# Hybrid decoder layer on Trainium2: forgetting attention with its pools opened once, keys loaded by block on SP's queue, output-projection tiles laid singly between its items, and casts on other engines

## The chip, the cores and the metric

One core of a Trainium2 chip runs the whole program. The metric is device time in microseconds (us), from runs of the unchanged kernel: median 3135.35 of three (3137.12, 3130.89, 3135.35). Engines are named as in the profile: PE (TensorE matmul), PEld (its weight load), DVE (VectorE), ACT (ScalarE), POOL (GpSimd), SP (SyncE, which here only issues transfers). ACTq and SPq are the streams of transfers that ACT and SP issue. TensorE's clock has two levels, 1.2 and 2.4 GHz; the profile prints the granted share, 0.5 to 1.0.

## The reference, cut to what matters

One layer, 2048 positions, width 1024. Four groups of heads (RWKV-7, mLSTM, sliding-window attention, forgetting attention) read one normalised input; their outputs stand side by side in `y` (2048 x 1024) and one output projection maps them back. The change touches the last group and that projection.

```
def _fox(z, b_f):                       # 4 heads of 64
    q, k, v, f_pre = split(z)
    c = cumsum(log_sigmoid(f_pre + b_f), axis=1)
    s = q_i . k_j / 8 + c_i - c_j       # j <= i, else -inf
    return softmax(s) @ v

y = concatenate([y_a, y_b, y_c, y_d])
x = x + rmsnorm(y @ w_out, norm_mix_post)
h = rmsnorm(x, norm_ffn_pre)
gate, up = split(h @ ffn_w_up)          # then conv, GELU, product, w_down, rmsnorm, residual
```

## The kernel before

**Stages.** `stage1` does the input projection and the RWKV heads, and as fillers beside them the other groups. `stage2` does forgetting attention ("fox") and the output projection. `stage_n` does the channel mixer: the up products (L1580), then the down product. Positions are cut into NC = 4 chunks of C = 512 and these into 4 sub-tiles of 128 rows, so there are 16 tiles t; chunk c holds tiles 4c to 4c+3.

**Fox items.** An item is (head h, chunk c of queries). The order, number by number, is 0, 1: heads 0, 1 of chunk 0; 2, 3: heads 0, 1 of chunk 1; 4, 5: heads 2, 3 of chunk 0; 6, 7: heads 2, 3 of chunk 1; 8 to 11: chunk 2; 12 to 15: chunk 3. An item has a front and a back. The front (`fox_front`, L1281) loads queries and the c+1 key blocks of 512 (`fox_load`, L1264: tiles `ka` and `kb`), forms the logits for 128 queries and a block at a time (L1291, L1292, and L1294 for the mask), takes the minimum on DVE (L1295), and ends in a transposition of the row minima (L1308) that ACT copies into `QB` (L1309). It has 4(c+1) steps. The back (`fox_back`, L1312) forms transposed logits for 128 keys a step (L1324, L1325, L1327), exponentiates on ACT (L1329, tile `fP`), splits the result into two halves of 16 bits (L1331 the rounded one, on ACT; L1333 the rest, on POOL for every third step and on DVE for the others; tile `fhl`), and multiplies with the values two steps later (L1339). It has 4(c+1)+2 steps. `fox` (L1364) interleaves the back of one item with the front of the next; with `first=True` the front of its first item runs alone, before anything of its back.

**Pools.** Fox's pools are opened twice: for items 0 to 5 with 5 key buffers and 2 PSUM banks for logits, and for items 6 to 15 with 8 key buffers and 4 banks. After item 5 the iterator of items is empty, so no front runs beside item 5's back.

**Output tiles.** `o_front` (L1435) loads 128 rows of `y` on SP (L1440), takes their maximum (L1442), splits into 16-bit halves in tile `hl` (L287, L288) and transposes these by transfers on SP (L290, `yt`). `o_back` (L1451) loads a tile of `x` on ACT's queue into the single buffer `xr` (L1456), runs 96 matmuls of 256 columns (L276 to L278), normalises (L1464 to L1469), adds `x` on POOL (L1470), stores it (L1471), and makes the transposed input of the channel mixer, `V` (L298, L301, L284, L285, L290), through the same two buffers `hl`. V of chunks 0 and 1 lies in a pool on the right side of SBUF; V of chunks 2 and 3 in a pool on the left that takes the memory of fox's pools when these close. `combine(0)` (L1475) then forms sums and differences of V of chunks 0 and 1 on POOL, DVE and ACT (L1485 to L1489, tile T0, in the same left pool); the first up product needs them and the first weights `Wup` (L1562, L1563).

**What sets the order.** Each engine runs its own instructions in a fixed order, and each of SP, ACT and POOL issues its transfers in that order too. The order is made at compile time (L1736): program order is the priority, and a simulated timeline lets later work go ahead where earlier work isn't ready. So L888 to L891 put tiles 0 to 3 behind item 7 and tiles 4 to 7 behind item 11, and L905 tiles 8 to 15 behind all of fox, but where they run is read from the trace.

Of the kernel before, what the change touches and what calls it, by code (L numbers as in the profile page):

```python
# [22 lines left out]
NC = T // C  # L23
# [116 lines left out]
class Trunk:  # L140
# [723 lines left out]
    def stage2(self):  # L864
        with ExitStack() as ck, ExitStack() as co:
            self.cr_.close()
            self.fk = self.pool(ck, "fk")
            items = [[(h, c) for h in hs] for c, hs in ((0, (0, 1)), (1, (0, 1)), (0, (2, 3)), (1, (2, 3)), (2, range(4)), (3, range(4)))]
            with ExitStack() as cf:
                self.fox_pools(cf, 5, 3, 5, 2)  # L870
                self.fox_setup()
                self.fox_items = iter(items[0] + items[1] + items[2])
                self.fox(3, True)
                self.fill_heads(1)
                self.fox(3)
            self.twice = False
            self.cm_.close()
            self.cf.close()
            self.cu.close()
            with ExitStack() as cf:  # L880
# [12 lines left out]
            keep = self.pool(self.ctx, "keep_n")  # L893
# [5 lines left out]
            self.sn = self.pool(self.ctx, "small_n", bufs=4)  # L899
# [333 lines left out]
    def fox_pools(self, ctx, nk, npe, nh, nps):  # L1233
# [3 lines left out]
        self.psf = self.pool(ctx, "ps_a", bufs=nps, space=PSUM)  # L1237
        self.fbufs = nk, npe, nh
# [25 lines left out]
    def fox_load(self, hp, c):  # L1264


        nc, wk = self.nc, self.fw
        qa, qb = wk.tile([P, C], F32R, name="qa", bufs=2), self.QB[self.loads % 3]
        self.loads += 1
        nc.scalar.dma_start(out=qa.bitcast(F32), in_=self.qF[hp][c][:, :])  # L1270
        nc.scalar.dma_start(out=qb[0:64].bitcast(F32), in_=self.qF[hp][c][0:64])
        nc.gpsimd.memset(qb[64:66].bitcast(F32), 0.0)
        K = []
        for b in range(c + 1):
            ka, kb = wk.tile([P, C], F32R, name="ka", bufs=self.fbufs[0]), wk.tile([68, C], F32R, name="kb", bufs=self.fbufs[0])
            nc.scalar.dma_start(out=ka.bitcast(F32), in_=self.kA[hp][b][:, :])
            nc.scalar.dma_start(out=kb.bitcast(F32), in_=self.kB[hp][b][:, :])
            K.append((ka, kb))
        return qa, qb, K

    def fox_front(self, hp, c):  # L1281

        nc, small, psf = self.nc, self.sf, self.psf
        qa, qb, K = self.ops = self.fox_load(hp, c)
        mx = small.tile([P, NSUB, 4], F32, name="fmx", bufs=3)
        for i in range(NSUB):
            isl = slice(i * P, (i + 1) * P)
            for b in range(c + 1):
                n = C if b < c else (i + 1) * P
                ps = psf.tile([P, C], F32, name="psf")  # L1290
# [15 lines left out]
        ps = psf.tile([P, C], F32, name="psf")  # L1306
# [5 lines left out]
    def fox_back(self, hp, c, ops):  # L1312

        nc, wk, small, psf = self.nc, self.fw, self.sf, self.psf
# [5 lines left out]
        def num(s):  # L1320
            b, ks = s // NSUB, slice(s % NSUB * P, s % NSUB * P + P)
            o = max(0, s - 4 * c) * P
            ps = psf.tile([P, C], F32, name="psf")
# [7 lines left out]
            nc.scalar.copy(out=h[:, 0, o:], in_=e[:, o:])  # L1331
            eng = nc.gpsimd if s % 3 == 1 else nc.vector
# [53 lines left out]
    def o_setup(self, ctx):  # L1386
        nc = self.nc
        self.U2 = [self.u2p.tile([P, 2, KT, C], F16, name=f"V{c}") for c in range(2)] + [None] * (NC - 2)
# [15 lines left out]
    def o_tiles(self, c):  # L1404
        if c == 0:
            self.of = self.o_front(0)
        for t in range(c * NSUB, (c + 1) * NSUB):
            self.of = self.o_back(t, self.of, t + 1 if t + 1 < NC * NSUB else None)
# [331 lines left out]
```

## Time and profile before

| what | us |
|---|---|
| median of three runs | 3135.35 |
| the profiled execution, whole | 3123.52 |
| its span, first to last instruction | 3121.4 |
| PE busy in the span | 2751.2 |
| from the last matmul of item 5 to the back of item 6 | 28.7 |
| fox from there to its end | 339.3 |
| from the end of fox to the first up product | 123.8 |

The profiled execution lies 11.8 us under the median of the runs. The spans of the last three lines are read from the timeline of PE; the rows stand below. A row of a timeline gives start and duration in us, engine, line, operation, output and inputs, and in brackets how long the engine had been idle and what released it.

### The profile page before, as it was taken

How to read it: one execution, taken by the hardware profiler on the slowest of the kernel's cores; microseconds unless marked ns; L12 is line 12 of the kernel's file. 1: busy time of each engine (PE TensorE's matmuls, PEld its weight loads, DVE VectorE, ACT ScalarE, POOL GpSimd, SP SyncE). 2: the span in 40 equal slices, each digit the busy share in tenths (PEclk: the TensorE clock that was granted, in tenths of full speed). 3: DMA queues.
4: the chain of work that ended last, by engine and by line, in shares of the span. 5: the costliest groups of instructions: out<-in, count | busy, mean ns of one | idle time of the engine just before them, and what ended most of it. 6: DMA issues, size and time to landing. Idle time of an engine off the chain costs nothing.

```text
span 3121.4 us, 45097 instructions
## 1 busy us (share of the span) xinstructions
PE 2751.2 (88%) x17374; PEld 1656.7 (53%) x17374; DVE 1707.9 (55%) x3512; ACT 1043.6 (33%) x1844; POOL 848.8 (27%) x989
## 2 busy tenths in 40 slices
PE   1499889999998989699885578999999998999998
PEld 0145577777776876577664233444444443444443
DVE  3465466557775655466766576466555554622120
ACT  2343222345452223356673322222222222522020
POOL 1153221223323332122224333333323332010110
PEclk9699889999988998799997799999999999999999
DMA  6441223244652365484425332111111111832120
GB/s 178 98 115 58 83 72 106 81 106 129 166 130 78 90 171 169 119 169 118 129 63 133 102 121 87 49 68 56 53 54 61 54 55 43 275 124 92 56 85 21
DMA packets 341398, 313.67 MB, mean 100 GB/s; under 512 B 217600, under 2 KB 271232, under 8 KB 338368
## 3 DMA queue, kind: packets, MB, share of 16 engines
q1 hardware_dynamic: 265856, 238.42, 27.2%
q10 hardware_dynamic: 75328, 72.39, 7.7%
q8 instruction: 136, 2.23, 0.3%
q14 instruction: 78, 0.64, 0.1%
HBM read 187.86 MB, written 89.56 MB: 89 GB/s over the span
## 4 chain that ended last, share of the span: by engine, by line
PE 47%; issue 11%; DVE 9%; DMA 8%; POOL 5%; ACT 1%; SPq 0%; ACTq 0%; POOLq 0%; DVEq 0%
PE psd L1675 10%; PE psb L1580 7%; PE psc L1580 4%; PE psa L1580 4%; PE pso L1339 1%; POOL S L1539 1%; DMA rd<-in_w_dn 1%; PE psf L276 1%; PE psf L278 1%; PE psf L277 1%; PE psf L268 1%; POOL F L1617 1%; PE psf L266 1%; PE psf L267 1%; PE psg L276 1%
## 5 line engine op out<-in xcount | busy, mean ns | idle before, releaser
L1580 PEld LDWEIGHTS <-Wup 128*128 128x128 f16 x3696 | 365.9, 99 | 537.8 <-issue 86.0
L1675 PE MATMUL psd<-Wd,f 128*128 128x512 f16 x2112 | 458.1, 380 | 8.2 <-ACT Wd L1660 8.1
L1580 PE MATMUL psb<-T,Wup 128*128 128x512 f16 x1584 | 382.6, 391 | 49.0 <-DVE up L1583 44.2
L1675 PEld LDWEIGHTS <-f 128*128 128x128 f16 x2112 | 207.0, 98 | 259.3 <-issue 6.6
L1580 PE MATMUL psa<-V,Wup 128*128 128x512 f16 x1056 | 248.8, 383 | 28.8 <-ACT Wup L1562 23.7
L276 PE MATMUL psg<-Wo,yt 128*128 128x256 f16 x512 | 145.7, 285 | 57.1 <-DMA yt<-hl 54.5
L1595 ACT ACTIVATE X<-psa,wm 128x512 f32<-128x512 f32 x44 | 30.2, 687 | 414.8 <-DVE p L205 244.3
L266 PE MATMUL psg<-U,hi_cm 128*128 128x512 f16 x256 | 103.8, 405 | 73.5 <-ACT hi_cm L253 73.5
L268 PE MATMUL psf<-U,lo_fm 128*128 128x256 f16 x576 | 161.5, 280 | 0.0
L266 PE MATMUL psf<-U,hi_fm 128*128 128x256 f16 x576 | 161.5, 280 | 0.0
L267 PE MATMUL psf<-U,hi_fm 128*128 128x256 f16 x576 | 161.4, 280 | 0.0
L278 PE MATMUL psg<-Wo,yt 128*128 128x256 f16 x512 | 143.7, 283 | 7.5 <-DMA yt<-hl 7.5
L277 PE MATMUL psg<-Wo,yt 128*128 128x256 f16 x512 | 145.7, 285 | 0.0
L1619 DVE TENSOR_REDUCE mF<-F 128x2 f32<-128x1024 f32 x44 | 53.7, 1221 | 165.7 <-POOL F L1617 165.6
L276 PE MATMUL psf<-hi_fv,U 128*128 128x256 f16 (+1 forms) x512 | 137.8, 276 | 3.6 <-ACT zc L779 3.6
L1683 DVE TENSOR_SCALAR od<-psd,sf 128x512 f32<-128x512 f32 x16 | 12.0, 750 | 233.6 <-PE psd L1675 229.1
L277 PE MATMUL psf<-lo_fv,U 128*128 128x256 f16 (+1 forms) x512 | 138.1, 276 | 0.0
L278 PE MATMUL psf<-hi_fv,U 128*128 128x256 f16 (+1 forms) x512 | 137.8, 276 | 0.0
L1580 PE MATMUL psc<-T,Wup 128*128 128x512 f16 x528 | 131.9, 381 | 0.0
L1295 DVE TENSOR_REDUCE fmx<-psf 128x1 f32<-128x512 f32 (+3 forms) x160 | 96.0, 606 | 64.8 <-PE psf L1292 38.8
L268 PE MATMUL psg<-U,lo_cm 128*128 128x512 f16 x256 | 102.4, 401 | 32.5 <-DVE lo_cm L254 18.7
L1329 ACT ACTIVATE fP<-psf,ln2k 128x512 f32<-128x512 f32 (+3 forms) x160 | 97.5, 624 | 78.3 <-PE psf L1325 31.5
(446 smaller groups left out, 5979.5 us busy)
## 6 DMA issues: line engine op xcount, KB each, us to landing
raw<-in_w_up SPq DMA_DIRECT2D x22, 1024.0 KB
fD<-F SPq DMA_DIRECT2D x44, 512.0 KB
fr<-fD SPq DMA_DIRECT2D x88, 256.0 KB
rd<-in_w_dn SPq DMA_DIRECT2D x22, 512.0 KB
wdr<-in_w_dn ACTq DMA_DIRECT2D x22, 512.0 KB
zin<-zR SPq DMA_DIRECT2D x80, 128.0 KB
ka<-kA ACTq DMA_DIRECT2D x40, 256.0 KB
wst<-in_w_cm SPq DMA_DIRECT2D x17, 512.0 KB
```

Of the source, the lines that this page charges most:

```text
L266: nc.tensor.matmul(ps[:, sl], lhsT=hi[:, k, n0:n0 + nn], rhs=uh[:, k, sl], start=k == 0, stop=False)
L267: nc.tensor.matmul(ps[:, sl], lhsT=hi[:, k, n0:n0 + nn], rhs=ul[:, k, sl], start=False, stop=False)
L268: nc.tensor.matmul(ps[:, sl], lhsT=lo[:, k, n0:n0 + nn], rhs=uh[:, k, sl], start=False, stop=k == KT - 1)
L276: nc.tensor.matmul(ps, lhsT=uh[:, k, sl], rhs=hi[:, k, n0:n0 + nn], start=k == 0, stop=False)
L277: nc.tensor.matmul(ps, lhsT=uh[:, k, sl], rhs=lo[:, k, n0:n0 + nn], start=False, stop=False)
L278: nc.tensor.matmul(ps, lhsT=ul[:, k, sl], rhs=hi[:, k, n0:n0 + nn], start=False, stop=k == KT - 1)
L1295: nc.vector.tensor_reduce(out=mx[:, i, b:b + 1], in_=ps[:, :n], axis=AX.X, op=ALU.min)
L1329: nc.scalar.activation(out=e[:, o:], in_=ps[:, o:], func=AF.Exp, scale=-1.0, bias=self.ln2k)
L1339: nc.tensor.matmul(po[i // 2][:, i % 2 * 129:i % 2 * 129 + 129], lhsT=h[:, n, i * P:(i + 1) * P], rhs=self.V2[:, s, hp], start=s == 0 and ...
L1580: nc.tensor.matmul(ps, lhsT=W[:, a, n, ks], rhs=rhs[u](b, k), start=first and k == 0 and i == 0, stop=k == 3 and i == 2, skip_group_check= ...
L1619: nc.vector.tensor_reduce(out=self.mF[:, 2 * p:2 * p + 2, j:j + 1], in_=F, axis=AX.X, op=ALU.max, apply_absolute_value=True)
L1675: nc.tensor.matmul(ps, lhsT=f[:, a, sl], rhs=Wd[j][:, b, ns], start=j == 0 and k == 0, stop=j == NF - 1 and k == 2)
```

## The change

Fox's pools are opened once, for all items, with 6 key buffers; two more PSUM banks are added as a second pool once the fillers' pools close, and `fox_bank` takes banks from the two in turn. Items come from one iterator, so item 6's front runs beside item 5's back. `o_setup` (weights of the output projection, 16 loads on SP) moves ahead of items 3 to 5.

In `fox_front` the loop over key blocks becomes the outer one, and block b+1 is loaded when block b starts, on SP's queue instead of ACT's; queries stay on ACT's queue.

Of the back's steps, every third rounds on DVE instead of ACT, and every second one (before: every third) takes the rest on POOL instead of DVE.

Output tiles are laid between items: tile 0 ahead of item 6, 1 ahead of 7, 2 ahead of 8, 3 ahead of 9, 4 and 5 ahead of 10, 6 ahead of 11, none ahead of 12, 7 ahead of 13, 8 ahead of 14, 9 ahead of 15, and 10 to 15 behind all of fox. Where the second argument is given, the next tile's front isn't begun within this one's back. V of chunk 2 moves to the right-hand pool. `combine(0)` moves from behind tile 11 to behind tile 15.

```
     def stage2(self):
-            items = [[(h, c) for h in hs] for c, hs in (...)]
-            with ExitStack() as cf:
-                self.fox_pools(cf, 5, 3, 5, 2)
+                items = [(h, c) for c, hs in (...) for h in hs]
+                self.fox_pools(ck, 6, 4, 6)
                 self.fox_setup()
-                self.fox_items = iter(items[0] + items[1] + items[2])
+                self.fox_items = iter(items)
                 self.fox(3, True)
                 self.fill_heads(1)
+                self.twice = False
+                self.cm_.close()
+                self.cf.close()
+                self.cu.close()
+                self.psfs.append(self.pool(ck, "ps_a1", bufs=2, space=PSUM))
+                self.u2p = self.pool(self.c2, "u2", side="right")
+                self.o_setup(co)
                 self.fox(3)
-            self.twice = False
-            self.cm_.close()
-            self.cf.close()
-            self.cu.close()
-            with ExitStack() as cf:
-                self.fox_pools(cf, 8, 4, 6, 4)
-                self.u2p = self.pool(self.c2, "u2", side="right")
-                self.fox_items = iter([i for l in items[3:] for i in l])
-                self.fox(1, True)
-                self.o_setup(co)
-                self.fox(1)
-                for c in range(1, NC):
-                    if c > 1:
-                        self.fox(4)
-                    if c <= 2:
-                        self.o_tiles(c - 1)
-            ck.close()
+                for n, t in ((1, ((0,),)), (1, ((1,),)), (1, ((2,), 2)), (1, ((3,), 3)), (1, ((4,5),)), (1, ((6,),6)), (1, ((),)), (1, ((7,), 7)), (1, ((8, ),8)), (1, ((9,),9))):
+                    self.o_tiles(*t)
+                    self.fox(n)
...
-            for c in range(2, NC):
-                self.U2[c] = u2b.tile([P, 2, KT, C], F16, name=f"V{c}")
+            self.U2[NC - 1] = u2b.tile([P, 2, KT, C], F16, name="V3")
...
-            for c in range(2, NC):
-                self.o_tiles(c)
-                if c == 2:
-                    self.combine(0, lambda n: self.ow.tile([P, 4, W], F32, name="xs"), self.Tc[0])
+            self.o_tiles(range(10, 16), 15)
+            self.combine(0, lambda n: self.ow.tile([P, 4, W], F32, name="xs"), self.Tc[0])
...
+        def more():
+            b = len(K)
+            ka, kb = ...
+            nc.sync.dma_start(out=ka.bitcast(F32), in_=self.kA[hp][b][:, :])
+            nc.sync.dma_start(out=kb.bitcast(F32), in_=self.kB[hp][b][:, :])
+            K.append((ka, kb))
+        more()
+        return qa, qb, K, more
+    def fox_bank(self):
+        self.turn += 1
+        return self.psfs[self.turn % len(self.psfs)].tile([P, C], F32, name="psf")
...
     def fox_front(self, hp, c):
         for b in range(c + 1):
-            nc.scalar.dma_start(out=ka.bitcast(F32), in_=self.kA[hp][b][:, :])
-            nc.scalar.dma_start(out=kb.bitcast(F32), in_=self.kB[hp][b][:, :])
...
-        for i in range(NSUB):
-            for b in range(c + 1):
+            if b < c:
+                more()
+            for i in range(NSUB):
...
     def fox_back(self, hp, c, ops):
-            nc.scalar.copy(out=h[:, 0, o:], in_=e[:, o:])
-            eng = nc.gpsimd if s % 3 == 1 else nc.vector
+            if s % 3 == 2:
+                nc.vector.tensor_copy(out=h[:, 0, o:], in_=e[:, o:])
+            else:
+                nc.scalar.copy(out=h[:, 0, o:], in_=e[:, o:])
+            eng = nc.gpsimd if s % 2 == 1 else nc.vector
             eng.tensor_tensor(out=h[:, 1, o:], in0=e[:, o:], in1=h[:, 0, o:], op=ALU.subtract)
...
     def o_setup(self, ctx):
-        self.U2 = [... for c in range(2)] + [None] * (NC - 2)
+        self.U2 = [... for c in range(NC - 1)] + [None]
```

## Rows read from the trace of the kernel before

**Rows 1.** The page: the span, and the busy time of PE and DVE with their shares.

```profile
span 3121.4 us, 45097 instructions
...
PE 2751.2 (88%) x17374; PEld 1656.7 (53%) x17374; DVE 1707.9 (55%) x3512; ACT 1043.6 (33%) x1844; POOL 848.8 (27%) x989
```

**Rows 2.** Busy time of each engine in seven stretches. Columns: stretch, its length, busy us (and instructions) of PE, PEld, DVE, ACT, POOL, granted clock, share of the DMA engines, GB/s.

```profile
1216.00:1265.60 49.60, 39.37 (x243) 26.19 (x241) 22.32 (x64) 24.16 (x52) 8.52 (x11) 0.73 0.52 162
1265.60:1294.30 28.70, 8.75 (x26) 5.38 (x26) 11.87 (x30) 2.46 (x3) 0.00 (x0) 0.50 0.88 199
1294.30:1633.60 339.30, 314.33 (x2608) 243.23 (x2606) 231.97 (x447) 211.39 (x391) 94.38 (x85) 0.95 0.49 117
1633.60:1651.60 18.00, 0.01 (x1) 0.01 (x1) 10.32 (x18) 5.43 (x6) 4.95 (x7) 0.53 0.91 209
1651.60:1757.40 105.80, 59.51 (x481) 49.09 (x481) 62.12 (x93) 36.69 (x58) 46.25 (x50) 0.77 0.46 114
1757.40:1900.00 142.60, 108.28 (x447) 45.51 (x448) 97.97 (x109) 32.62 (x31) 44.11 (x49) 0.88 0.35 119
1900.00:2650.00 750.00, 715.71 (x3251) 320.40 (x3249) 414.01 (x455) 203.96 (x195) 252.62 (x192) 0.98 0.15 54
```

**Rows 3.** Timeline of PE where the pools change: the end of item 5's back, the first logits of item 6's front, the start of its back.

```profile
1264.36 1.26 PE L1339 MATMUL pso<-FV,fhl 128*128 128x129 f16 x10 [1.20 <-POOL fhl L1333]
1274.48 0.77 PE L1291 MATMUL psf<-ka,qa 128*128 128x512 f32 x1 [8.85 <-DMA ka<-kA]
1276.74 0.77 PE L1292 MATMUL psf<-kb,QB 68*128 68x512 f32 x1 [1.50 <-DMA kb<-kB]
...
1294.19 1.87 PE L1308 MATMUL psf<-c,fmr 128*2 128x128 f32 x8
```

**Rows 4.** Transfers issued on ACT's queue and on SP's around it (start, time the issue took, queue, line).

```profile
1217.11 21.12 SPq L1399 DMA_DIRECT2D Wo<-wO  x16
...
1267.65 0.48 ACTq L1270 DMA_DIRECT2D qa<-qF  x1
1268.17 0.44 ACTq L1276 DMA_DIRECT2D ka<-kA  x1
...
1576.72 0.36 ACTq L1276 DMA_DIRECT2D ka<-kA  x1
1577.15 0.32 ACTq L1277 DMA_DIRECT2D kb<-kB  x1
```

**Rows 5.** Starts of the backs of items 12 to 15 on PE (L1308 comes once an item).

```profile
1498.55 1.03 PE L1308 MATMUL psf<-c,fmr 128*2 128x128 f32 x8 [0.63 <-DVE fmr L1305]
1542.24 1.03 PE L1308 MATMUL psf<-c,fmr 128*2 128x128 f32 x8
1581.56 1.03 PE L1308 MATMUL psf<-c,fmr 128*2 128x128 f32 x8
1613.07 1.03 PE L1308 MATMUL psf<-c,fmr 128*2 128x128 f32 x8 [1.31 <-DVE fmr L1305]
```

**Rows 6.** What PE waited for from 1296 to 1634, the values' matmuls (L1339): us in total, times, longest.

```profile
PE pso L1339 <- DVE fhl L1333: 4.6, 7, 1.2
...
PE pso L1339 <- POOL fhl L1333: 3.6, 4, 1.8
```

**Rows 7.** Groups by line from 1296 to 1634: the split's instructions on DVE, ACT and POOL by shape, and one line of the tiles' matmuls. Columns: count, busy us, mean ns of one, idle before.

```profile
L1333 DVE TENSOR_TENSOR fhl<-fP,fhl 128x512 f16<-128x512 f32 x66 | 56.0, 855 | 15.2 <-ACT fhl L1331 15.1
L1331 ACT CAST fhl<-fP 128x512 f16<-128x512 f32 x98 | 58.8, 621 | 3.7 <-DVE fmx L1295 1.6 <-POOL xr L1470 0.8
L1333 POOL TENSOR_TENSOR fhl<-fP,fhl 128x512 f16<-128x512 f32 x32 | 41.2, 1287 | 121.4 <-ACT fhl L1331 109.7 <-issue 5.1 <-PE psf L1325 3.9
L278 PE MATMUL psg<-Wo,yt 128*128 128x256 f16 x352 | 98.2, 281 | 0.8 <-DMA yt<-hl 0.8
```

**Rows 8.** A stretch of SP's stream in the middle of fox, and its first rows after fox's end.

```profile
1448.17 31.99 SPq L290 DMA_TRANSPOSE V<-hl  x4
...
1637.14 0.32 SPq L1440 DMA_DIRECT2D y<-ybuf  x1
1637.63 3.49 SPq L290 DMA_TRANSPOSE V<-hl  x2
```

**Rows 9.** PE and ACT at the end of fox: the last fox matmuls, the first tile matmul behind them, and ACT's split of the row before it.

```profile
1632.09 0.75 PE L1339 MATMUL pso<-FV,fhl 128*128 128x129 f16 x10 [0.47 <-POOL fhl L1333]
1651.59 0.40 PE L276 MATMUL psg<-Wo,yt 128*128 128x256 f16 x1 [18.75 <-DMA yt<-hl]
...
1643.15 1.15 ACT L287 ACTIVATE hl<-y,p 128x1024 f16<-128x1024 f32 x1 [7.37 <-DMA V<-hl]
```

**Rows 10.** Loads of `x` for the last three tiles on ACT's queue, and POOL's add of the last one.

```profile
1712.45 0.34 ACTq L1456 DMA_DIRECT2D xr<-in_x  x1
1729.11 0.34 ACTq L1456 DMA_DIRECT2D xr<-in_x  x1
1742.67 0.34 ACTq L1456 DMA_DIRECT2D xr<-in_x  x1
...
1746.92 2.34 POOL L1470 TENSOR_TENSOR xr<-xr,o 128x1024 f32<-128x1024 f32 x1 [2.13 <-DMA xr<-in_x]
```

**Rows 11.** `combine(0)`: its instructions over the whole trace (duration ns min/median/max, first and last start us).

```profile
L1485 POOL TENSOR_TENSOR xs<-V x32: 658/665/1652, 1368.1 to 1715.8; 128x256 f32<-128x256 f16 x32
L1489 DVE TENSOR_TENSOR T<-xs,T x8: 1219/1225/1226, 1635.8 to 1722.5; 128x1024 f16<-128x1024 f32 x8
```

**Rows 12.** What PE waited for from 1757 to 1900: us in total, times, longest.

```profile
PE psa L1580 <- ACT Wup L1562: 23.7, 3, 15.4
PE psb L1580 <- DVE up L1583: 16.7, 4, 9.3
```

More of the change, by code (lines that the diff above doesn't have):

```diff
@@ L864, in stage2 @@
     def stage2(self):
[L865 removed]
+        with ExitStack() as co:
             self.cr_.close()
[L867 to L870 removed]
+            keep = self.pool(self.ctx, "keep_n")
+            self.sn = self.pool(self.ctx, "small_n", bufs=4)
+            with ExitStack() as ck:
+                self.fk = self.pool(ck, "fk")
+                items = [(h, c) for c, hs in ((0, (0, 1)), (1, (0, 1)), (0, (2, 3)), (1, (2, 3)), (2, range(4)), (3, range(4))) for h in hs]
+                self.fox_pools(ck, 6, 4, 6)
                 self.fox_setup()
[L872 removed]
+                self.fox_items = iter(items)
                 self.fox(3, True)
                 self.fill_heads(1)
[L875 to L893 removed]
+                self.twice = False
[5 more added lines that the diff above has]
+                self.o_setup(co)
+                self.fox(3)
+                for n, t in ((1, ((0,),)), (1, ((1,),)), (1, ((2,), 2)), (1, ((3,), 3)), (1, ((4,5),)), (1, ((6,),6)), (1, ((),)), (1, ((7,), 7)), (1, ((8, ),8)), (1, ((9,),9))):
+                    self.o_tiles(*t)
+                    self.fox(n)
             self.row(keep, "post2")
@@ L1230, in swa_chunk, with fox_pools @@
             f = g
-    def fox_pools(self, ctx, nk, npe, nh, nps):
+    def fox_pools(self, ctx, nk, npe, nh):
         self.fw = self.pool(ctx, "fw", bufs=2)
@@ L1236, in fox_pools @@
         self.pso = self.pool(ctx, "ps_o", bufs=2, space=PSUM)
-        self.psf = self.pool(ctx, "ps_a", bufs=nps, space=PSUM)
+        self.psfs, self.turn = [self.pool(ctx, "ps_a", bufs=2, space=PSUM)], 0
         self.fbufs = nk, npe, nh
@@ L1273, in fox_load, with fox_front @@
         K = []
-        for b in range(c + 1):
-            ka, kb = wk.tile([P, C], F32R, name="ka", bufs=self.fbufs[0]), wk.tile([68, C], F32R, name="kb", bufs=self.fbufs[0])
-            nc.scalar.dma_start(out=ka.bitcast(F32), in_=self.kA[hp][b][:, :])
-            nc.scalar.dma_start(out=kb.bitcast(F32), in_=self.kB[hp][b][:, :])
[L1278 to L1285, printed above, removed]
-        for i in range(NSUB):
-            isl = slice(i * P, (i + 1) * P)
-            for b in range(c + 1):
+        def more():
+            b = len(K)
+            ka, kb = wk.tile([P, C], F32R, name="ka", bufs=self.fbufs[0]), wk.tile([68, C], F32R, name="kb", bufs=self.fbufs[0])
+            nc.sync.dma_start(out=ka.bitcast(F32), in_=self.kA[hp][b][:, :])
[6 more added lines that the diff above has]
+        return self.psfs[self.turn % len(self.psfs)].tile([P, C], F32, name="psf")
+    def fox_front(self, hp, c):
+        nc, small = self.nc, self.sf
+        qa, qb, K, more = self.fox_load(hp, c)
+        self.ops = qa, qb, K
+        mx = small.tile([P, NSUB, 4], F32, name="fmx", bufs=3)
+        for b in range(c + 1):
+            if b < c:
+                more()
+            for i in range(NSUB):
+                isl = slice(i * P, (i + 1) * P)
                 n = C if b < c else (i + 1) * P
-                ps = psf.tile([P, C], F32, name="psf")
+                ps = self.fox_bank()
                 nc.tensor.matmul(ps[:, :n], lhsT=qa[:, isl], rhs=K[b][0][:, :n], start=True, stop=False)
@@ L1305, in fox_front @@
         nc.vector.tensor_tensor(out=mr[:, 1], in0=mn, in1=mr[:, 0].bitcast(F32), op=ALU.subtract)
-        ps = psf.tile([P, C], F32, name="psf")
+        ps = self.fox_bank()
         for i in range(NSUB):
@@ L1312, in fox_back @@
     def fox_back(self, hp, c, ops):
-        nc, wk, small, psf = self.nc, self.fw, self.sf, self.psf
+        nc, wk, small = self.nc, self.fw, self.sf
         qa, qb, K = ops
@@ L1322, in num @@
             o = max(0, s - 4 * c) * P
-            ps = psf.tile([P, C], F32, name="psf")
+            ps = self.fox_bank()
             nc.tensor.matmul(ps[:, o:], lhsT=K[b][0][:, ks], rhs=qa[:, o:], start=True, stop=False)
@@ L1387, in o_setup @@
         nc = self.nc
-        self.U2 = [self.u2p.tile([P, 2, KT, C], F16, name=f"V{c}") for c in range(2)] + [None] * (NC - 2)
+        self.U2 = [self.u2p.tile([P, 2, KT, C], F16, name=f"V{c}") for c in range(NC - 1)] + [None]
         self.so = self.small = self.pool(ctx, "small_o", bufs=2, side="right")
@@ L1402, in o_setup, with o_tiles @@
         self.of = None
[L1404 to L1408, printed above, removed]
+    def o_tiles(self, ts, last=None):
+        for t in ts:
+            if self.of is None:
+                self.of = self.o_front(t)
+            self.of = self.o_back(t, self.of, t + 1 if t != last else None)
     def o_weights(self, sp):
```

1 line of the change is left out of this document (removed).

## The prediction

> **What bounds the kernel now.** The page first: PE is busy 88% of the span and DVE 55% [rows 1]. An average over stages, so I cut the timeline at the places that the change touches and read busy time stretch by stretch [rows 2]. From 1900 us on the up products keep PE busy 95% of the time at almost full clock; nothing there changes. Fox between 1294.3 and 1633.6 is bound by PE as well: 314.3 of 339.3 us, clock 0.95, so at most some 25 us of idle time and a little clock can be won. The losses lie on either side. Between 1265.6 and 1294.3 PE is busy for 8.75 of 28.7 us, at the lower clock level (granted 0.50, which is 1.2 GHz). From 1633.6 to the first up product at 1757.4 it is busy for 59.5 of 123.8 us. So I read who ended the waits in these two places.
>
> At the first, the last matmul of item 5 ends at 1265.6, the first logits of item 6 start at 1274.5 when `ka` lands, and item 6's back starts at 1294.2 [rows 3]. The queries for it were issued at 1267.65, the first keys at 1268.17 [rows 4]: the pools had just changed, no front had run ahead, and everything started cold. At the second, the y rows of tile 12 are loaded at 1637.1, right behind them come four transpositions of V for tiles 8 and 9 [rows 8], which have been waiting for memory that fox's pools held, ACT's split waits for them because they hold `hl`, and PE starts on a tile at 1651.6 after 18.75 us [rows 9]. From there five tiles follow, one after another: counted by one of three matmul lines at 32 a tile, eleven tiles have run inside fox [rows 7] although only eight were written ahead of its end, so five are left. Their spacing is set by the one buffer for `x`: the last three loads are 16.7 and 13.6 us apart [rows 10], and the add on POOL starts 4.25 us after the load's issue, so load, add, norm and split follow one another without overlap. Over all five the spacing is (1742.7 - 1651.6)/5 = 18.2 us, since `combine(0)` takes turns with them on POOL and DVE [rows 11].
>
> **The change part by part.** The sum is made against the profiled execution, 3123.5 us (span 3121.4 and 2.1 around it). It lies 11.8 us under the median of the runs, 3135.35; I take the difference from the sum and apply it to the median.
>
> *Pools opened once.* Item 6's front now runs beside item 5's back. The stretch of 28.7 us goes; what it contained, 8.75 us of PE at the lower level, is 4.4 us at the upper, and remains. In the 49.6 us before, PE is idle for 10 us [rows 2], which hides it. Gain 28.7 - 4.4 = 24.3. Bounds: 29 if it is all hidden; 10 if SP loads item 6's keys no earlier than ACT did, because the 16 weight loads, 21 us long on SP's stream [rows 4], go ahead of them: then only one block has to arrive (6.8 us from issue to first use [rows 3, 4]) instead of a whole cold front. The weights end at 1238, ten us or more before they are needed in item 5's back, so I take 24.
>
> *Keys on SP's queue, by block.* Issuing a pair costs ACT 0.36 + 0.32 us [rows 4]. For the 32 pairs of items 6 to 15 and the 8 before this is 27 us of ACT's stream, which is not the bound (211 of 339 us busy [rows 2]): worth nothing. The Trainium skill ("DMA: Bandwidth & Descriptors", Issuing engines are not separate DMA queues) says that transfers from any engine share the same DMA engines and that another issuer saves only the issue time; by it too this part would bring no more than those 27 us of ACT, and on the path nothing. What it may cost is on SP. A block is now asked for four front steps ahead of its use. Items of chunk 3 take 43.7, 39.3 and 31.5 us [rows 5] for 16 front steps, so four steps are 8 to 11 us; a load took 6.8 cold. It fits, by 1 to 4 us. Behind a waiting SP instruction stand key loads, and behind these PE. Central 0; the cost if it doesn't fit is a rival. Six key buffers instead of eight hold for the same reason: the seventh block is asked for as the first is given up.
>
> *Casts.* Of the 128 back steps in the stretch some 43 roundings leave ACT (0.62 us each) for DVE, and POOL takes 64 rests instead of 42. DVE loses 22 of these (0.86 each, 19 us) and gains 43 roundings, at no more than a rest's 0.86 and no less than half of it: net 0 to +18 us on 232 of 339. POOL gains 22 x 1.29 = 28 us on 94 [rows 2, 7]. Neither becomes the bound. On the path lies what PE waits for: 3.6 us for rests from POOL and 4.6 for those from DVE [rows 6]. With half again as many on POOL the first becomes 5.5: +2 us. Bounds -4 (both waits halve through the lighter ACT) and +28 (each added POOL rest is waited for in full).
>
> *Tiles laid singly; V of chunk 2 on the right.* Ten tiles are laid among the items and two more (10, 11) can run ahead, now with memory for their V: tile 11 moves into fox. A tile is 59.5/5 = 11.9 us of PE, part of it at the lower clock; fox has 25 us of idle PE, and I take half the tile as hidden: +5 us (0 to +12). Tiles whose front isn't begun early (3, 4, 7 to 9) need load, maximum, split and transposition first, with an item's matmuls to cover it.
>
> *The tail.* The 18 us between the last fox matmul and the first tile matmul stay: tile 12 needs the last item's output and then the same chain. Tiles 12 to 15 remain: four at between 13.6 and 18.2 us, 16 each, 64 us instead of 91. From the last x load to the first up product: 14.7, as before. Tail 18 + 64 + 14.7 = 97 instead of 124: -27. Bounds -37 (13.6 a tile) and -4 (`combine(0)`, now behind tile 15, runs after it).
>
> The up products that follow wait for weights and DVE [rows 12]; none of that changes. The earlier items 0 to 5 get two more PSUM banks late and one more buffer; 0.
>
> Sum: -24 + 0 + 2 + 5 - 27 = -44. 3135.4 - 44 = **3091**.
>
> **The rivals.**
> 1. *`combine(0)` comes last.* Its 32 adds on POOL take 32 x 0.665 = 21 us and DVE's part ends a little later [rows 11]: 22 us behind tile 15 ahead of the first up product. For it: the program puts it there, and in this trace it took turns with tiles 11 to 15 because it stood between them. Against: its inputs are ready when fox ends, and POOL is idle for over half of 105.8 us [rows 2]. It gives -44 + 22 = -22: 3113.
> 2. *Keys behind SP's waits: slower.* SP also carries y loads and transpositions, in fixed order, and sat for 32 us over four transpositions in the middle of fox [rows 8]. If key loads are placed behind such waits, the front's matmuls, and everything on PE behind them, come late. Items 8 to 15 have 4 x 2 + 4 x 3 = 20 blocks that are asked for only one block ahead. It decides against the change from 44/20 = 2.2 us a block; at 3.5, a tenth of that wait, it is +70: 3161. Against it: the same planner orders SP's stream by its simulated time, and in before it placed ACT's key loads just as narrowly.
> 3. *DVE and POOL lock each other out.* In fox DVE's rests average 855 ns and POOL's 1287 [rows 7]; with 22 more on POOL, each holding DVE up in full and PE behind it, the casts cost 28 instead of 2: 3117. DVE is idle for 107 of 339 us, which speaks against. The Trainium skill ("SBUF — State Buffer", Who interferes with whom) states that the two share a port pair under an exclusive lock; nothing in these rows separates that from ordinary waiting.
> 4. *It doesn't do what it says.* The planner had already moved eleven tiles into fox, and the laying only displaces them: six fronts that aren't begun early leave PE short, the cold start's gain is eaten, or two of the rivals come together: 3135, within 6.
>
> **How the numbers follow.** Forecast 3091 (3065 to 3108): 0.58. Rival 1: 0.15. Rival 2: 0.13. Rival 3: 0.06. Rival 4: 0.08. The lower end is all lower bounds: -29 - 4 + 0 - 37 = -70, 3065. The upper is 3128, which takes in rivals 1 and 3 with some 11 us above the latter, and leaves out 2 and 4, 0.21. What a measurement of this kernel can tell from no change is about 0.2%, 6 us. Faster: 0.58 + 0.15 + 0.06 = 0.79; within: 0.08; slower: 0.13.
>
> **What would show it.** Cold start: the back of item 6 should begin within some 3 us of item 5's last matmul, and no wait of PE for `ka` over 2 us. Keys: waits of PE for `ka` and `kb` in fox in sum under 5 us; over 40 would make the prediction wrong on the slow side. Casts: waits of PE for `fhl` under 12 us. Tiles: 12 tiles' matmuls ahead of fox's end, and PE over 93% busy in fox. Tail: four tile matmul groups after the last fox matmul, first up product some 97 us behind it; some 120 means rival 1, with `T` written after the last transposition of V. If the stages from 1900 on differ by more than some us, the sum has missed a term.

## The result and the profile after

The changed kernel takes 3173.55 us (median of four, 3158.7 to 3182.23) where the kernel before takes 3133.12 in the same comparison: ratio 1.0123, 95% interval 1.0083 to 1.0163. It is 1.2% slower; 3091 was forecast. The profiled execution took 3158.7 us, 15 under its median. From the page of the changed kernel, the span and PE's line [rows 1]:

```profile
span 3156.8 us, 45169 instructions
PE 2758.0 (87%) x17374; PEld 1662.5 (53%) x17374; DVE 1715.6 (54%) x3532; ACT 1018.2 (32%) x1796; POOL 878.3 (28%) x1017
```

Busy time of each engine of the changed kernel in eight stretches (columns as in [rows 2]): stage 1, up to the back of item 6, to fox's end, to the first up product, three of the channel mixer's up to the first down product, the down product:

```profile
0.00:1100.00 1100.00, 919.24 (x7178) 656.10 (x7179) 649.21 (x1922) 376.76 (x885) 305.61 (x508) 0.91 0.40 104
1100.00:1284.40 184.40, 167.94 (x1300) 133.36 (x1298) 98.08 (x285) 55.70 (x109) 55.22 (x73) 0.93 0.63 174
1284.40:1638.00 353.60, 317.21 (x2570) 244.73 (x2571) 243.80 (x479) 192.44 (x351) 123.20 (x105) 0.94 0.52 124
1638.00:1766.30 128.30, 65.88 (x523) 53.65 (x521) 76.09 (x116) 42.04 (x67) 52.88 (x58) 0.79 0.40 111
1766.30:1900.00 133.70, 100.84 (x409) 42.25 (x410) 94.09 (x104) 32.51 (x31) 43.67 (x48) 0.87 0.36 118
1900.00:2650.00 750.00, 717.47 (x3260) 321.49 (x3258) 413.41 (x447) 202.54 (x194) 247.11 (x191) 0.98 0.14 54
2650.00:2674.80 24.80, 6.67 (x31) 2.84 (x29) 12.29 (x19) 6.07 (x7) 5.06 (x3) 0.70 0.42 141
2674.80:3156.80 482.00, 462.71 (x2112) 208.07 (x2111) 128.62 (x163) 110.13 (x154) 45.53 (x32) 0.98 0.30 102
```

The kernel before, in the stretches that answer to the first, the second to fourth (its own bounds; its last fox matmul ends at 1632.8, 0.8 us ahead of the cut in [rows 2]) and the last:

```profile
0.00:1100.00 1100.00, 939.43 (x7341) 671.48 (x7341) 660.95 (x1947) 380.80 (x893) 313.55 (x517) 0.91 0.40 106
1100.00:1294.20 194.20, 155.71 (x1140) 119.91 (x1139) 96.12 (x277) 57.53 (x112) 44.91 (x59) 0.84 0.62 166
1294.20:1632.80 338.60, 314.39 (x2609) 243.31 (x2608) 231.21 (x443) 211.03 (x390) 94.38 (x85) 0.95 0.49 117
1632.80:1757.40 124.60, 59.55 (x482) 49.10 (x481) 73.20 (x115) 42.49 (x66) 51.20 (x56) 0.74 0.52 127
2652.00:3121.40 469.40, 458.12 (x2112) 206.90 (x2111) 132.77 (x167) 113.17 (x157) 48.01 (x33) 0.99 0.32 109
```

And the line that opens the back of every item, over the whole trace (durations, first and last start): before, then after.

```profile
L1308 PE MATMUL psf<-c,fmr x128: 269/273/421, 1156.1 to 1613.8; 128*2 128x128 f32 x128
```

```profile
L1309 PE MATMUL psf<-c,fmr x128: 272/272/273, 1163.6 to 1610.7; 128*2 128x128 f32 x128
```

Cut at such points, the 35.4 us between the two profiled spans are spread over the whole program:

| stretch | before | after | difference |
|---|---|---|---|
| start to the back of item 0 | 1156.1 | 1163.6 | +7.5 |
| to the back of item 6 | 138.1 | 120.8 | -17.3 |
| to fox's end | 338.6 | 353.6 | +15.0 |
| to the first up product | 124.6 | 128.3 | +3.7 |
| to the last up product's end | 888.5 | 891.2 | +2.7 |
| to the first down product | 6.1 | 17.3 | +11.2 |
| down product | 469.4 | 482.0 | +12.6 |

Only the second line is a gain. Two of the losses lie in stages whose code the change doesn't touch: stage 1 (PE did 20 us less in its first 1100) and the down product.

### The profile page after: what moved, and what is told of

Its sections match the earlier page's. It is cut to its first block, busy times and chain, and to the rows that moved or that the text cites. A ratio compares the mean times of both kernels' runs of the same rounds, so it can differ in the third digit from the quotient of the medians.

```text
span 3156.8 us, 45169 instructions
## 1 busy us (share of the span) xinstructions
PE 2758.0 (87%) x17374; PEld 1662.5 (53%) x17374; DVE 1715.6 (54%) x3532; ACT 1018.2 (32%) x1796; POOL 878.3 (28%) x1017
## 5 line engine op out<-in xcount | busy, mean ns | idle before, releaser
L1679 PE MATMUL psd<-Wd,f 128*128 128x512 f16 x2112 | 462.7, 383 | 27.4 <-ACT Wd L1664 27.4
L1337 POOL TENSOR_TENSOR fhl<-fP,fhl 128x512 f16<-128x512 f32 (+1 forms) x80 | 91.8, 1151 | 177.6 <-ACT fhl L1335 121.8
```

The source lines that it names most:

```text
L1337: eng.tensor_tensor(out=h[:, 1, o:], in0=e[:, o:], in1=h[:, 0, o:], op=ALU.subtract)
L1679: nc.tensor.matmul(ps, lhsT=f[:, a, sl], rhs=Wd[j][:, b, ns], start=j == 0 and k == 0, stop=j == NF - 1 and k == 2)
```

## The experiments

All times are medians; the ratio is to the kernel before on the same chip. The first four ran together, and so did 5 to 8, 9 to 12 and 13 to 15.

**1. The down product's buffers (e1, e2, e5).** PE's wait for the first weights of the down product, us in total, times, longest; before, then after:

```profile
PE psd L1675 <- ACT Wd L1660: 8.1, 3, 6.1
```

```profile
PE psd L1679 <- ACT Wd L1664: 27.4, 3, 17.3
```

Behind it stands ACT's load and split of these weights. Before, the first load goes out 45 us ahead of the last up product's end (2645.9):

```profile
2600.93 0.34 ACTq L1658 DMA_DIRECT2D wdr<-in_w_dn  x1
...
2650.82 1.13 ACT L1660 ACTIVATE Wd<-wdr,sd 128x1024 f16<-128x1024 f32 x1
```

After, it goes out 6 us ahead of it (2657.5), and a later split waits for the store of `F` to leave the memory that its load goes to:

```profile
2651.06 0.45 ACTq L1662 DMA_DIRECT2D wdr<-in_w_dn  x1
2673.09 0.82 ACTq L1662 DMA_DIRECT2D wdr<-in_w_dn  x2
...
2679.92 1.15 ACT L1664 ACTIVATE Wd<-wdr,sd 128x1024 f16<-128x1024 f32 x1 [5.16 <-DMA fD<-F]
```

The reading: V of chunk 2 (16 KB of each partition) left the pool `u2b` at the bottom of the stack. `ffn_down` lays 64 KB of weights over `u2b` (64 KB before, 48 after), and `s0`, `wb` and `st` behind them. So everything behind slid 16 KB up against the buffers of the up products: `s0` from `raw` and `S`, given up early, to `Wup`, needed to the end.

e1, four tiles moved behind `s0`:

```
-Wd = [None] * 3 + [wa.tile(...) for j in range(3, 19)]
+Wd = [None] * 3 + [wa.tile(...) for j in range(3, 15)]
-Wd = [wb.tile(...) for j in range(3)] + Wd[3:] + [wb.tile(...) for j in range(19, NF)]
+Wd = [wb.tile(...) for j in range(3)] + Wd[3:] + [wb.tile(...) for j in range(15, NF)]
```

> The changed kernel, but with four of the down product's weight tiles (Wd15 to Wd18, 16 KB of a partition) taken from the pool behind instead of the pool in front, so that the buffers of its first loads lie again over raw and S, which are given up early, and not over Wup, which is in use until the last up product. Theory (moving V of chunk 2 to the right pushed these buffers 16 KB up): the waits of PE for the first Wd go from 27 us back to about 8, the down product from 472 to about 460; 23 to 33 us under the changed kernel, so 3140 to 3150, about level with before. Rival (the late transition is a consequence of what goes before it, or of the lower clock): within 5 us of the changed kernel, 3168 to 3178.

Measured: 3169.03, ratio 1.0141 (1.0111 to 1.0172): nothing gained on the change's 1.0123. The first load was early again, but the first down product still came 13.0 us after the up products and took 480.4. As it stood, the theory had failed; but four tiles in `wb` push `st` up by the same 16 KB, and a split still waited 6.13 us for the store of `F`.

e2, the shift alone in the kernel before (`range(3, 22)` in `wa`, 12 KB):

> The kernel before, with nothing changed but that three more of the down product's weight tiles (12 KB of a partition) are taken from the pool in front, so that its first loads' buffers lie over Wup as in the changed kernel. Theory: first down product some 15 to 20 us later, the down product some 10 us longer, 3155 to 3168 in all. Rival (the place in memory is without effect): 3130 to 3138, as before.

Measured: 3134.55 against 3125.25, ratio 1.0024 (1.0004 to 1.0044): 7.5 us to the first down product instead of 6.1, and 475.7 for it instead of 469.4. The place has a price; with 12 KB it is 9 us, where 30 to 43 were expected.

e5, the four tiles in a pool opened last, so that `s0`, `wb`, `st` and `f` lie where they lay:

```
 small = self.pool(ctx, "small_d", bufs=4)
+wc = self.pool(ctx, "wc_d")
-... + Wd[3:] + [wb.tile(...) for j in range(19, NF)]
+... + Wd[3:] + [wc.tile(...) for j in range(15, 19)] + [wb.tile(...) for j in range(19, NF)]
```

> The changed kernel, with the four weight tiles Wd15 to Wd18 of the down product moved to a pool opened last, so that every one of its other buffers (the first loads' and those of the loads that follow) lies over the same stage-n buffers as in the kernel before; the first experiment put only the very first ones back and pushed the others 16 KB over F's. Theory (place in memory decides the late transition and the slow start of the down product): waits of PE for Wd back to some 8 us, the down product from 481 to about 469 us; some 18 us under the first experiment, 3145 to 3158 where the kernel before takes 3125 to 3135. Rival (what comes late is the order that the planner gives to the loads, wherever the buffers lie): within 5 us of the first experiment, ratio to before 1.012 to 1.016, down product 478 or more.

Measured: 3144.99, ratio 1.0063 (1.0037 to 1.0090); 5.8 us to the first down product, 469.7 for it, and the wait:

```profile
PE psd L1680 <- ACT Wd L1665: 7.2, 2, 5.8
```

Both are what they were before. The place of the buffers is the cause of the loss behind the up products, shown. It is worth 0.6% against the change (1.0123 to 1.0063) and 0.8% against e1; in the two profiles of the table it is 23.8 us, 0.8%.

**2. Stage 1 (e6).** The first instruction that differs between the two programs on SP's stream is the load of the mask, `fneg` in `fox_setup`: one of 64 KB, issued at 1111.8 us before and at 16.4 after (duration min/median/max, first and last start; before, after, and e6):

```profile
L1246 SPq DMA_DIRECT2D fneg<-in_cst x1: 460/460/460, 1111.8 to 1111.8; - x1
```

```profile
L1236 SPq DMA_DIRECT2D fneg<-in_cst x1: 328/328/328, 16.4 to 16.4; - x1
```

```profile
L1236 SPq DMA_DIRECT2D fneg<-in_cst x1: 754/754/754, 1112.0 to 1112.0; - x1
```

Its pool is opened above fox's, which are larger now and stand above `keep_n` and `small_n`; so it lies, as the early issue tells, in memory that is free in stage 1, and the planner issues it at once. From there its order of stage 1 differs on every engine, though that code is the same. e6:

```
-self.fox_pools(ck, 6, 4, 6)
-self.fox_setup()
+self.fox_setup()
+self.fox_pools(ck, 6, 4, 6)
```

> The changed kernel with two lines changed round: fox_setup ahead of fox_pools, so that the small pool with the mask (64 KB in all) lies again over memory of stage 1 and its load can't run at 16 us. Every engine's order in stage 1 is then that of the kernel before, up to fox's first loads. Theory (the changed order of stage 1 costs the late start of fox): the back of item 0 begins at some 1156 us instead of 1164 to 1178, PE is busy some 20 us more up to 1100, and the whole is 8 to 20 us under the changed kernel, ratio to before 1.006 to 1.010. Rival (item 0 is late because of the loads of keys on SP): item 0 stays at 1164 or later, ratio 1.012 or more.

Measured: 3141.10, ratio 1.0051 (1.0030 to 1.0072), where the change has 1.0123. By the traces PE runs its first 7,495 matmuls in the order of the kernel before, where the change leaves that order after 1,580. PE is busy for 943.77 us of the first 1100 (939.43 before, 919.24 after). The back of item 0 starts at 1163.3, no earlier than after, so this sign of the theory (1156) failed; but that of item 6 starts at 1264.9, 19.5 us earlier: filler work that stage 1 had left undone had run between the first items (784 matmuls from item 0 to item 6 after, 714 in e6). The later runs bear this out: items 0 to 6 take 119.6 to 127.8 us in the five kernels that load the mask at 16 us (the change, e1, e3, e4, e5) and 100.6 to 105.3 in the nine with the setup first (e6 to e14). Shown is that the order costs 0.7%; whether the planner reacted to the one load or to the pools' places isn't separated.

**3. The tiles (e3, e10, e11).** e3 is e1 with the tiles placed as before:

```
-for n, t in (...):
-    self.o_tiles(*t)
-    self.fox(n)
+self.fox(2); self.o_tiles(range(0, 4)); self.fox(4); self.o_tiles(range(4, 8)); self.fox(4)
...
-self.o_tiles(range(10, 16), 15)
-self.combine(0, ...)
+self.o_tiles(range(8, 12)); self.combine(0, ...); self.o_tiles(range(12, 16), 15)
```

> The first experiment's kernel with the output tiles placed as in the kernel before: tiles 0 to 3 behind item 7, 4 to 7 behind item 11, 8 to 11, then the combine, then 12 to 15 behind fox, each tile's front begun within the one before it. Theory (laying the tiles singly, several with a fresh front, is what keeps PE waiting for yt, 61 us from item 6 on, and leaves five tiles behind fox): fox ends 10 to 15 us earlier or holds one more tile, and it takes 15 to 30 us off the first experiment, 3115 to 3130. Rival (the late start of items 0 to 5, the keys or the casts cost it): within 5 us of the first experiment.

Measured: 3139.85, ratio 1.0053 (1.0030 to 1.0075), 0.9% under e1; four tiles behind fox instead of five and a half.

e10 and e11 stand on e8 (below; ratio 0.9886) and differ in one thing: whether a tile's front is begun within the tile before it. e10 has the change's list of tiles, e11 the same without the second arguments; both keep the combine behind tile 11.

```
-... (1, ((2,), 2)), (1, ((3,), 3)), ... (1, ((6,),6)), ... (1, ((7,), 7)), (1, ((8, ),8)), (1, ((9,),9))
+... (1, ((2,),)), (1, ((3,),)), ... (1, ((6,),)), ... (1, ((7,),)), (1, ((8, ),)), (1, ((9,),))
```

> The same kernel with the tiles laid singly between the items as in the change, six of them with a fresh front, and the combine left behind tile 11. Theory (laying costs what it did between the first and the third experiment, some 28 us, by fronts not begun early and a tile less in fox; the combine's place costs little of that): ratio 0.996 to 0.999, five tiles behind fox. Rival (the combine behind tile 15 was the cost): within 6 us of the kernel with three undone and the casts as before.

> As the experiment before it, but each tile's front is begun within the tile before, also across items. Theory (the fresh fronts cost it: load, maximum, split and transposition ahead of each tile's matmuls with PE waiting for yt): most of the loss comes back, ratio 0.988 to 0.992. Rival (the places between the items cost it, since a tile stands in front of an item's first steps): ratio stays at 0.996 or more.

Measured: e10 3136.64, ratio 1.0009 (0.9989 to 1.0030); e11 3099.08, ratio 0.9887 (0.9860 to 0.9913). Six second arguments cost 1.2%, more than was expected of them in e10. The places between the items cost nothing that the ratios show (0.9887 against e8's 0.9886, each to within 0.4%); in the profiles they move time, from item 6 to fox's end 347.6 us instead of 338.5 for the same twelve tiles, and 112.0 instead of 114.9 behind it. From the back of item 7 to fox's end (columns as in [rows 2]) and PE's waits for `yt` there, first e10, then e11:

```profile
1281.40:1640.80 359.40, 314.66 (x2484) 240.56 (x2485) 221.19 (x425) 199.00 (x373) 90.58 (x79) 0.91 0.49 115
PE psg L276 <- DMA yt<-hl: 13.5, 5, 3.8
PE psg L278 <- DMA yt<-hl: 13.5, 4, 5.1
```

```profile
1283.90:1613.40 329.50, 308.51 (x2606) 240.90 (x2606) 229.26 (x435) 204.67 (x385) 93.78 (x84) 0.96 0.56 132
PE psg L278 <- DMA yt<-hl: 3.7, 2, 3.2
PE psg L276 <- DMA yt<-hl: 3.1, 2, 1.9
```

Without the early front PE waits 27.0 us for `yt` instead of 6.8, its granted clock in this stretch is 0.91 instead of 0.96, and more than a tile less is done at the end of it.

**4. The keys' queue (e4, e9).** `nc.scalar.dma_start` for `ka` and `kb` in place of `nc.sync.dma_start`; e4 on e1, e9 on e8.

> The first experiment's kernel with the key blocks loaded on ACT's queue again, one block ahead as in the changed kernel. Theory (the keys cost nothing: PE waited for none of them): within 5 us of the first experiment. Rival (the key loads make SP issue the y loads and the transpositions of yt later): 8 to 20 us under it, with fewer waits of PE for yt.

> The experiment with three undone and the casts as before (3088 us, ratio 0.9886), with the key blocks loaded on ACT's queue again, still one block ahead. The fourth experiment had this beside a changed order of stage 1 and was 0.6% over the first, for reasons spread over stages that hold no keys. Theory (SP's queue for the keys is worth nothing by itself, since PE waits for no key block on either): within 5 us, ratio 0.987 to 0.990. Rival (ACT's issues delay its exponentials and roundings, 0.36 + 0.32 us a pair): 8 to 20 us over, ratio 0.991 to 0.995.

Measured: e4 3188.10, ratio 1.0198 (1.0169 to 1.0226), 0.6% over e1, which neither expectation has; but 22 of its 31 us more of span lie in the up products (912.4 instead of 890.0), which load no keys. e9, where stage 1 has the order of before: 3100.18, ratio 0.9880 (0.9852 to 0.9908), level with e8. Within these intervals the keys' queue is worth nothing by itself.

**5. The casts (e7, e8, e15).** e7 is e6 with the buffers of e5 and the tiles of e3; e8 is e7 with

```
-            if s % 3 == 2: nc.vector.tensor_copy(...)
-            else: nc.scalar.copy(...)
-            eng = nc.gpsimd if s % 2 == 1 else nc.vector
+            nc.scalar.copy(...)
+            eng = nc.gpsimd if s % 3 == 1 else nc.vector
```

and e15 is the kernel before with the reverse edit.

> All three undone at once: the setup first, the down product's buffers where they were, the tiles placed by chunk as before (combine behind tile 11). What is left of the change is pools opened once, keys by block on SP's queue, the casts, and V of chunk 2 on the right. Theory (the three hidden costs add up, 8 + 28 + 19 us, and the forecast gain of the cold start remains): faster than the kernel before by 5 to 15 us, ratio 0.995 to 0.998. Rival (what is left of the change brings nothing or costs): ratio 1.000 to 1.006.

> As the experiment with all three undone, and with the casts as in the kernel before too: every rounding on ACT, every third rest on POOL. Theory (the casts are worth nothing, since DVE, ACT and POOL all have room): within 3 us of it. Rival (the rests on POOL hold DVE and PE up): 5 to 15 us under it; the reverse (ACT was in the way): 5 to 10 over it.

> The kernel before with the new casts alone: every third rounding on DVE, every second rest on POOL. Theory (they cost what lay between the experiments with three undone and with the casts as before too, some 10 us): ratio 1.002 to 1.005, with more waits of PE for the split's halves in fox. Rival (that difference was the planner's order of what lies around them): ratio 0.998 to 1.001.

Measured: e7 3098.18, ratio 0.9924 (0.9896 to 0.9953), better than either expectation; e8 3088.36, ratio 0.9886 (0.9849 to 0.9923); e15 3135.98 against 3123.46, ratio 1.0048 (1.0029 to 1.0067). In the kernel before the casts cost 12.5 us; e7 against e8 has 9.8, with intervals that overlap. From the back of item 6 to fox's end e15 takes 348.4 us (1298.3 to 1646.7) instead of 338.6. PE is busy for 317.9 of them instead of 314.4, so its waits are 6.2 us longer, and these are spread: in sum 10.3 us instead of 8.4 for `fhl` and 4.8 instead of 2.8 for `yt`. The longest in e15:

```profile
PE pso L1342 <- POOL fhl L1336: 5.5, 4, 4.7
PE psg L278 <- DMA yt<-hl: 4.6, 3, 2.9
```

The expected growth of the waits for `fhl` is there, but small, and no single wait explains the 12.5 us. The profiled run of e15 is also the slowest of its twelve, and 9.9 us of its longer span lie in the up products (898.4 instead of 888.5), which hold no casts. What the casts delay is not shown.

**6. Two buffers for x (e12).** On e8: `name="xr", bufs=2`, and `fox_pools(ck, 6, 3, 6)` for the room.

> The kernel with three undone and the casts as before, with two buffers for the tile xr instead of one; to make room there are three buffers for fP instead of four. Theory (the prediction's: the single buffer for x sets the spacing of the tiles behind fox, 16 us each, as load, add, norm and split follow one another): the spacing of the four tiles behind fox falls from 19 us, 10 to 20 us less in all, ratio 0.982 to 0.986. Rival (the tiles' spacing is set by something else, as the shared buffers hl, o and the combine between them): within 5 us.

Measured: 3115.64, ratio 0.9944 (0.9921 to 0.9966), slower than e8. Fox's end to the first up product takes 111.7 us instead of 114.9. The adds of the four tiles behind fox are 17.4, 22.8 and 16.3 us apart in e8 and 17.4, 23.5 and 10.1 in e12. The last add, e8 and then e12:

```profile
1704.87 2.34 POOL L1474 TENSOR_TENSOR xr<-xr,o 128x1024 f32<-128x1024 f32 x1 [6.49 <-DMA xr<-in_x]
```

```profile
1713.63 3.20 POOL L1474 TENSOR_TENSOR xr<-xr,o 128x1024 f32<-128x1024 f32 x1 [1.45 <-issue]
```

So the single buffer for `x` sets the last spacing only, some 6 us; for the others the prediction's reason is wrong. The loss lies elsewhere: item 6 to fox's end takes 345.3 instead of 338.5, with one buffer of `fP` less, and the up products 912.4 instead of 894.3, as in e4, with more waits of PE for `up`; why isn't settled.

**7. The change mended (e13, e14).** The change whole, with three mends: `fox_setup` first (e6), the four tiles in `wc` (e5), no second arguments (e11). e14 moves the combine behind tile 11 as well.

> The change whole, with three mends only: the setup ahead of the pools, the down product's four tiles in a pool opened last, and each tile's front begun within the tile before. Tiles stay laid singly, the new casts, the keys on SP and the combine behind tile 15 stay. Theory (the three are the whole of the miss, the casts cost some 10 us): ratio 0.990 to 0.994. Rival (the combine behind tile 15 costs too, up to 22 us by its adds): ratio 0.995 to 1.000.

> As the first of this call, with the combine behind tile 11 instead of 15. Theory (the planner moves its instructions early anyway): within 5 us of it. Rival (its place costs): 10 to 20 us under it.

Measured: e13 3095.00 against 3123.46, ratio 0.9911 (0.9886 to 0.9936); e14 3099.00, ratio 0.9930 (0.9905 to 0.9955). The three make up 2.1% of the 2.6% between the forecast (3091, ratio 0.986) and the change (1.0123), and the combine's place costs nothing that shows. Best of all is e8 (0.9886), with e9 and e11 level. e14 and e11 differ in the casts alone: their ratios are 0.9930 and 0.9887, on two chips, but their medians (3099.00, 3099.08) and their times from item 6 to fox's end (348.2, 347.6) are the same. So with the tiles laid singly, what the casts cost isn't settled.

## Why the prediction was wrong

The step that failed is that only fox and its tail were costed: "nothing there changes" from 1900 us on, nothing at all on stage 1, and "with an item's matmuls to cover it" for the tiles without an early front. The three sums that were missing or too small are 0.6% (the down product's buffers), 0.7% (the order of stage 1) and 1.2% (fronts not begun early), some 78 us together by single experiments; undone together they bring 1.0123 to 0.9911, 66 us. The prediction gave "slower" a chance of 0.13, but by rival 2, which did not happen. The last sentence of the prediction named the sign, stages from 1900 on that differ; the diff held the reason (a tile moved out of a pool that another stage's pools are laid over), and the prediction didn't follow it into `ffn_down`.

*Point by point*, in e13, where the change can be seen without the three (spans, item 0's back at 1158.8):

```profile
1159.00:1259.40 100.40, 90.67 (x713) 68.58 (x712) 56.16 (x160) 39.83 (x83) 25.99 (x32) 0.93 0.62 174
1259.40:1606.80 347.40, 321.77 (x2708) 247.53 (x2708) 250.62 (x488) 197.46 (x363) 120.51 (x111) 0.98 0.55 132
1606.80:1719.50 112.70, 50.44 (x384) 40.90 (x384) 68.92 (x107) 36.42 (x55) 48.94 (x53) 0.72 0.43 107
```

- *Pools once*: -24 forecast, at most -29. Items 0 to 6 take 100.6 us (1158.8 to 1259.4) instead of 138.1: -37.5. The mechanism, a cold start that goes, was right and the size too small: PE's idle time in the stretch falls from 30.4 to 9.7 us, and its busy time from 107.7 to 90.9, with 54 matmuls fewer and a granted clock of 0.93 instead of 0.80. What the prediction did not read is that the last idle time before item 6's back was no wait for keys, but for the first output tile:

```profile
1293.23 0.39 PE L276 MATMUL psg<-Wo,yt 128*128 128x256 f16 x1 [9.60 <-DMA yt<-hl]
```

  In the unmended kernel the back of item 6 begins 17.3 us sooner after item 0's. No run has the pools without the rest.
- *Keys*: 0 forecast, and 0 by e9 for the queue; loading by block has no run of its own. In all of the changed kernel PE waited 0.6 us for a key, once, ahead of item 0's back, so rival 2 falls. This agrees with the Trainium skill ("DMA: Bandwidth & Descriptors", Issuing engines are not separate DMA queues): another issuer saves its issue time only, and 0.9880 against 0.9886, each to within 0.4%, shows not even that on the path.
- *Casts*: +2 forecast, with bounds -4 and +28; e15 has +12.5. Mis-sized in the kernel before, though inside its bounds; which wait it had wrong stays open, since those for `fhl` grow by 1.9 us only, as forecast. Rival 3 as it was priced, each added rest holding DVE up in full, doesn't hold: in e15 DVE's rests average 867 ns (855 before) and POOL's 1338 (1287), 54 x 12 ns + 44 x 51 ns, 2.9 us in all. The three DVE operations of the tiles on 128x1024 (1282, 1216 and 1321 ns before; 1543, 1400 and 1443 in e15) are 5.8 us longer over 31 instructions. How much of either comes from what the Trainium skill ("SBUF — State Buffer", Who interferes with whom) states, that the two share a port pair under an exclusive lock, no run here separates.
- *One more tile in fox*: with fronts begun early, twelve tiles run there. The twelfth costs nothing in e8 (338.5 us from item 6 on, with the old places and casts, where the kernel before has 338.6 with eleven). Laid singly it is 347.6 with the old casts (e11) and 347.4 with the new (e13): +8.8 where the two terms gave +7, but it is the price of the laying. Without early fronts ten and a half run, and it takes 353.6.
- *Tail*: -27 forecast, -11.9 measured in e13 (112.7 against 124.6). POOL's adds of the last four tiles in e13 (start, duration, and idle time with its releaser):

```profile
1654.71 3.21 POOL L1474 TENSOR_TENSOR xr<-xr,o 128x1024 f32<-128x1024 f32 x1 [1.46 <-ACT T L1492]
1673.32 2.34 POOL L1474 TENSOR_TENSOR xr<-xr,o 128x1024 f32<-128x1024 f32 x1 [0.96 <-DMA xr<-in_x]
1694.06 2.52 POOL L1474 TENSOR_TENSOR xr<-xr,o 128x1024 f32<-128x1024 f32 x1
1709.15 2.34 POOL L1474 TENSOR_TENSOR xr<-xr,o 128x1024 f32<-128x1024 f32 x1 [6.44 <-DMA xr<-in_x]
```

  The first add comes 47.9 us after fox's end, then three spacings of 18.1 in the mean, then 10.3 to the first up product. Before, the last of five adds is in [rows 10], and the four ahead of it are

```profile
1681.18 3.20 POOL L1470 TENSOR_TENSOR xr<-xr,o 128x1024 f32<-128x1024 f32 x1 [1.45 <-ACT T L1488]
1699.44 2.35 POOL L1470 TENSOR_TENSOR xr<-xr,o 128x1024 f32<-128x1024 f32 x1
1718.60 2.46 POOL L1470 TENSOR_TENSOR xr<-xr,o 128x1024 f32<-128x1024 f32 x1 [1.40 <-DVE o L1469]
1733.71 2.34 POOL L1470 TENSOR_TENSOR xr<-xr,o 128x1024 f32<-128x1024 f32 x1 [5.82 <-DMA xr<-in_x]
```

  so the first comes 48.4 us after fox's end, and the spacings are 16.4 in the mean. The prediction's 18.2 was misread: it divided a stretch that begins with the first tile's matmuls and ends with the last load. A tile less takes one spacing of 16.4 off, and the other three get wider, not narrower, by 1.7 each: the combine's `xs` adds still run on POOL between them, up to 1688.6 in e13 and 1694.7 in e14, wherever the program puts it. (The prediction's bound of -4 is -27 + 22, so -5.)
- *Rival 1* falls: the combine is done before the last tile's add in either place. *Rival 4* was the nearest: fronts that aren't begun early. It was priced at the loss of the gains, not beyond them.

Put together, e13 has +2.7 before item 0, -37.5, +8.8, -11.9, +1.8 in the up products and nothing behind them: 36.0 us under the span before, where -44 was forecast. By the medians it is 28.5 us (3123.46 to 3095.00), two thirds of the forecast; 0.9911 of 3135.35 is 3107, at the upper edge of 3065 to 3108. (The prediction also works out an upper end of 3128; the change's 3173.55 lies above both.) Without the three the direction holds and the size only in part, and that by luck too: the cold start gave 13.5 us more than forecast, the tail 15.1 less.

## What to carry to other kernels

When a diff moves a tile from one pool to another, follow the stack to every later pool that is laid over it, and ask which loads then lie over a buffer in use to the end; 16 KB cost 0.6 to 0.8%, in a later stage. Where a program orders itself at compile time, compare the streams from the first instruction on, not from the first changed line: one load that is suddenly early can be the first sign of a new order behind it, in which code that nobody touched gets slower. And where a step is split into a front and a back, an argument that stops the front from running ahead can cost more than where the step is put (here 1.2%, by 20 us more of waits for `yt` among others).

## What the runs showed of the hardware

- A late start costs more than its wait. The first down product of the changed kernel is 11.2 us late, and the down product then takes 12.6 longer: 8 of these in further waits for weights (27.4 - 17.3 us behind the first wait, 8.1 - 6.1 before), and 4.6 in a busier PE (462.7 and 458.1 us), whose granted clock is 0.70 in the stretch with the wait and 0.92 in the 100 us behind it, where the kernel before has 0.98.
- Runs of one kernel on one chip spread by 1% (e5: 3129.95 to 3164.65 in twelve; the kernel before beside it 3110.51 to 3143.3 in 24). One profile against another would not have told 0.4% from nothing; the ratios of many runs do.
